# The shared products of a paired down projection stored by ScalarE and summed DRAM to DRAM, the last pair in eight plain products, and an own weight buffer for the first block

## The chip, the cores and the metric

The kernel runs on one core of a Trainium2 chip. The metric is the device time of one execution in microseconds (us), and of several runs the median counts. Besides the timed runs there is one execution that the hardware profiler recorded; every duration of a single instruction below is from it.

## The reference

One layer of a bidirectional encoder, for a prompt of 256 tokens and a sample of 512 with the same weights. Three mixers (a state space model, differential attention, attention into a memory) are gated, projected and added to `x`; then a feed-forward part follows, and only that part is different in its order of work after the change.

```python
D_MODEL = 1024;  D_FF = 2816
def layer(x, mem, ...):
    h = rmsnorm(x, norm_mix_g)
    proj = h @ w_in
    ...                                   # s5_out, diff_out, mem_out
    br = jnp.einsum('blnc,ncd->blnd', branches, w_branch)
    merged = jnp.sum(gates * br, axis=2)
    x = x + merged @ w_out
    h2 = rmsnorm(x, ffn_norm_g)
    g, up = jnp.split(h2 @ w_gate_up, 2, axis=-1)
    return x + (jax.nn.silu(g) * up) @ w_down
```

All data are float32.

## The kernel before

**Precision.** A float32 operand of a matrix product is split into a high and a low part of a format that TensorE takes at a faster rate; ScalarE makes the high part by a copy, VectorE the low one by a subtraction. Each product is then three matmuls, high x high, low x high and high x low (helper `mm3`, lines 798 to 800). So every matmul of the kernel shows one of these three lines, and one tells the stages apart by the tiles' names.

**The feed-forward part.** The 768 tokens are worked as one. The 2816 hidden columns make 11 blocks of 256 (`NFB` = 11). Block 0 is computed plainly, segment by segment, while the normed rows of the last stage are still arriving: `first` (gate and up), then `down_first`, whose PSUM banks are added into the residual tiles `x1` (named `x_0` to `x_5`, one for 128 tokens; line 1486 before). The names there: `fa` is the block's activation, `hidh` its high part, `fs` a staging tile, `flo` the low part of the right factor T2.

Blocks 1 to 10 compute gate and up (`block`) by the Strassen-Winograd scheme: seven products of half-size matrices in place of eight. The sums of weight quarters for it (`ws`, then `wh_S`, `wl_S` after the split) are GpSimd's additions, lines 578 to 585, in `_split_w`. Their raw weights `wr` are loaded by SP into a pool of three tiles; the split halves `wh`, `wl` live in pools of four.

**The down projection in pairs.** The hidden blocks are taken two at a time, (1,2) to (9,10), so that the pair's 512 hidden rows can be cut in two as well and `down_pair` can use seven products (each 3 banks x 2 halves x 3 = 18 matmuls of 512 columns, tile `dn`). With A the activations (token halves by block) and B the weights, the left factors are A11, A12, A22 and the sums S1 to S4 (`ls`, and after the split `lS1h`, `lS1l` and so on, lines 1493 and 1494); the right ones are B11, B21, B22 and T1 to T4, which `_split_d` makes in two tiles `z` and `x` (named `wt...z`, `wt...x`) with ScalarE's negated copies and GpSimd's adding DMAs from `w_down`.

Four of the products go into one quarter of the output each. Three, A11·B11 ("1"), S2·T2 ("6") and S1·T1 ("5"), belong to several quarters. They are the same quarters in every pair, so these products are summed over the pairs in DRAM and added into `x1` once, in `down_sums` ahead of the last pair. On the way there, ScalarE copies a bank to a tile `de` (line 1543), and GpSimd issues the DMA (line 1549) that stores it, or from the second pair on adds it:

```python
gp.dma_start(p_scr[key][t], e[t], **({"accum_op": add} if fb > 1 else {}))
```

The `de` tiles come from a pool of three, which the tile `ft` of the gate's tanh uses too. In the last pair (`last`) there are no later sums: GpSimd issues twelve DMAs that add the `de` tiles straight into the residual tiles (`x<-de`, lines 1559 and 1574), and the output is stored from there by SP (line 1520).

**What sets the order.** A scheduler with a simulated timeline chooses the order of instructions on each engine. An engine then works its queue strictly in that order; a DMA that GpSimd issues stands in GpSimd's queue among its additions. Instructions marked with `keep_in_program_order` stay as written. Weights are fetched by a list (`W.add` fills it, `W.get` takes the next).

Of the kernel before, what the change touches and what calls it, by code (L numbers as in the profile page):

```python
# [487 lines left out]
TOK = 768  # L488
# [16 lines left out]
class WStream:  # L505
# [90 lines left out]
    def _split_d(self, i, h, kind):  # L596
# [16 lines left out]
        elif h == 0:  # L613
            add(self.x, b11)
            self._right(i, "T2", self.x)
            self._right(i, "T1", self.z)
            self._right(i, "B21", r)
        else:
            minus(self.x, self.x)
            add(self.x, b21)  # L620
            self._right(i, "T4", self.x)
            self._right(i, "B22", r)
# [47 lines left out]
def hybrid_block(ctx, tc, A, outs, consts):  # L670
# [48 lines left out]
    cp.tile([128, 32], F32, name="gapc")  # L719
# [41 lines left out]
    for fb in range(NFB):  # L761
        for what in ("gate", "up"):
            W.add(cols("w_gate_up", 256 * fb + (DFF if what == "up" else 0)), 8, 256, "w" if fb else None)
        if fb == 0:
            W.add(wd[:, 0:2, :], 2, 1024)
        elif fb % 2 == 0:
            for b, kind in ((fb - 1, "d"), (fb, "e")):
                W.add([wd[:, 2 * b : 2 * b + 2, 512 * c : 512 * c + 512] for c in range(2)], 4, 512, kind)


    def rsqrt(x, n, tag, bufs=4):
# [3 lines left out]
        y = sm.tile([128, n], F32, name=uid("rqy"), tag=tag, bufs=bufs)  # L775
# [101 lines left out]
    p_scr = {k: [dr.tile([128, 512], F32, name=f"p_scr{k}{t}") for t in range(3)] for k in "165"}  # L877
# [287 lines left out]
    def qk_units(h):  # L1165
        w = W.get()
        r = q2.tile([128, TILES, 256], F32, name=uid("qkraw"), tag="qkraw")
        ss = sm.tile([128, TILES * 4], F32, name=uid("qkss"), tag="qkss")
# [273 lines left out]
    def block(what, fb):  # L1442
# [29 lines left out]
        if what == "up" and fb % 2 == 0:  # L1472
            W.ahead(W.next + 1)
# [16 lines left out]
    def left(key, src):  # L1490
# [4 lines left out]
        L[key] = hi, lo  # L1495

# [6 lines left out]
    def down_begin(fb):  # L1503
# [3 lines left out]
        left("S3", left_sum(None, a[:, :, 0:HT], a[:, :, HT:TOK], sub))  # L1507
# [5 lines left out]
    def into(r, c, y, op=add, done=False, pin=False):  # L1513
        for t in range(3):
            o = out_block(r, c, t)
            i = v.tensor_tensor(out=o, in0=o, in1=y[t], op=op)  # L1516
            if pin:
                tc.keep_in_program_order(i)
# [3 lines left out]
    def down_pair(fb, last):  # L1522
# [8 lines left out]
        def prod(l, r):  # L1531
            (lh, ll), (rh, rl) = L.pop(l), R.pop(r)
            ps = [(psd if t else env.psb)("dn") for t in range(3)]
            for t in range(3):
                sl = slice(128 * t, 128 * t + 128)
                for k in range(2):
                    mm3(ps[t], lh[:, k, sl], ll[:, k, sl], rh[:, k], rl[:, k], k == 0, k == 1)
            return ps

        def copies(ps):  # L1540
            e = [ft_.tile([128, 512], F32, name=uid("de"), tag="ft") for t in range(3)]
            for t in range(3):
                act.activation(e[t], ps[t], AF.Copy)
            return e

        def keep(key, ps):
            e = copies(ps)
            for t in range(3):
                gp.dma_start(p_scr[key][t], e[t], **({"accum_op": add} if fb > 1 else {}))


        p1 = prod("A11", "B11")
# [3 lines left out]
        if last:  # L1556
            e = copies(p1)
            for t in range(3):
                gp.dma_start(out_block(0, 0, t), e[t], accum_op=add)
        else:  # L1560
            keep("1", p1)
        p7 = prod("S3", "T3")
        left("S1", s1)
        into(1, 1, p7, pin=last)
        if last:
            into(1, 0, p7)
        p6 = prod("S2", "T2")
        left("A12", a12)
        if last:
            for t in range(3):  # L1570
                v.tensor_tensor(out=e[t], in0=e[t], in1=p6[t], op=add)
            for r, c in ((1, 1), (1, 0), (0, 1)):
                for t in range(3):
                    gp.dma_start(out_block(r, c, t), e[t], accum_op=add)  # L1574
        else:
            keep("6", p6)
        p5 = prod("S1", "T1")
        left("A22", a22)
        left("S4", left_sum(s2, a12, s2, sub))
        if last:  # L1580
            into(0, 1, p5)
            into(1, 1, p5, done=True)
        else:
# [290 lines left out]
```

## Time and profile before

| what | value |
|---|---|
| runs | 1806.58, 1807.51, 1813.25 us; median 1807.51 |
| profiled execution | 1811.89 us, of which the span of instructions is 1810.1 |
| mean granted TensorE clock | 0.988 |
| block 0 of the feed-forward part | up to about 1347 us |
| the five pairs' `dn` windows begin at | 1391.8, 1480.2, 1572.6, 1665.4, 1755.6 us |
| the last matmul begins at | 1799.0 us |

Rows of the profile are read so. A row of an event has its start, its duration, engine, line, operation, and what it writes and reads (`out<-in`); in square brackets stands how long the engine had been idle and what ended that. A row of waits has the engine, the instruction that waited, after the arrow what it waited for, then the total time, the number of waits and the longest. A row of a window has its bounds, its length, and then for each engine (TensorE, its weight loads, VectorE, ScalarE, GpSimd, SyncE) the busy time and the number of instructions, then the mean granted clock (1.00 is full), the share of time in which the DMA engines moved data, and GB/s. If only one tile is asked for, the engines' columns hold that tile's instructions alone. `x3` behind an event means that three like ones follow one another.

### The profile page before, as it was taken

What the parts mean: (1) busy time and instruction counts of PE and PEld (TensorE: products, weight loads), DVE (VectorE), ACT (ScalarE), POOL (GpSimd) and SP (SyncE); (2) the same over time, 40 slices, a digit from 0 to 9 for tenths busy, and PEclk for the clock granted to TensorE, in tenths of its full rate; (3) what the DMA queues carried; (4) which work ended last, traced back from release to release, by engine and by line L of the source; (5) the groups of instructions that cost most, each with busy time, mean ns of one, the idle gap of its engine ahead of it and who ended that gap; (6) DMA issues with size and microseconds to landing.
All of it is one profiled execution on the core that took longest, in us unless ns stands there. A gap on an engine that the chain in (4) does not pass through costs nothing. (4 is left out here: it accounts for less than half of the span.)

```text
span 1810.1 us, 29578 instructions
## 1 busy us (share of the span) xinstructions
PE 1757.0 (97%) x11196; PEld 1615.4 (89%) x11196; DVE 1315.8 (73%) x2431; ACT 929.1 (51%) x1906; POOL 281.2 (16%) x308
## 2 busy tenths in 40 slices
PE   8999999999999989999999999999989999999986
PEld 8999988999999989999988888888879898989885
DVE  7655658799998678778865444434798787877786
ACT  7454544776666357777664442322435454444432
POOL 0000000000000011101100110000142525243532
PEclk9999999999999999999999999999999999999998
DMA  7232755665565487445932644321314355454656
GB/s 250 71 105 83 136 130 143 152 156 130 148 157 131 124 191 188 90 97 116 226 108 82 223 146 140 114 76 54 87 58 119 120 122 117 113 123 105 137 135 150
DMA packets 210430, 233.31 MB, mean 129 GB/s; under 512 B 59056, under 2 KB 168880, under 8 KB 210288
## 3 DMA queue, kind: packets, MB, share of 16 engines
q1 hardware_dynamic: 178512, 149.63, 27.9%
q0 software_dynamic: 30624, 78.66, 21.2%
q10 hardware_dynamic: 1152, 3.15, 0.5%
q8 instruction: 88, 1.44, 0.3%
q14 instruction: 54, 0.44, 0.1%
HBM read 158.96 MB, written 42.01 MB: 111 GB/s over the span
## 5 line engine op out<-in xcount | busy, mean ns | idle before, releaser
L638 ACT ACTIVATE wh<-wr 128x1024 fp32r<-128x1024 f32 x126 | 142.9, 1134 | 72.8 <-PE br L799 27.9
L644 DVE TENSOR_TENSOR wl<-wr,wh 128x1024 fp32r<-128x1024 f32 x80 | 106.5, 1332 | 74.3 <-ACT wh L638 73.2
L798 PE MATMUL gl<-Hhi,wh 128*128 128x256 f32 (+1 forms) x384 | 132.2, 344 | 1.3 <-ACT glt L1108 1.3
L800 PE MATMUL gl<-Hhi,wl 128*128 128x256 f32 (+1 forms) x384 | 128.9, 336 | 0.0
L799 PE MATMUL gl<-Hlo,wh 128*128 128x256 f32 (+1 forms) x384 | 128.8, 336 | 0.0
L642 POOL DMA_DIRECT2D wl<-wr x46 | 40.1, 871 | 519.2 <-ACT wl L641 484.0
L798 PE MATMUL qk<-wh,Hhi 128*128 128x256 f32 x384 | 108.7, 283 | 4.1 <-ACT qksq L1174 4.1
L799 PE MATMUL qk<-wl,Hhi 128*128 128x256 f32 x384 | 108.8, 283 | 0.0
L800 PE MATMUL qk<-wh,Hlo 128*128 128x256 f32 x384 | 108.8, 283 | 0.0
L798 PEld LDWEIGHTS gl<-Hhi,wh 128*128 128x128 f32 x384 | 72.2, 188 | 8.6 <-ACT glt L1108 1.5
L800 PEld LDWEIGHTS gl<-Hhi,wl 128*128 128x128 f32 x384 | 72.0, 188 | 8.1
L799 PEld LDWEIGHTS gl<-Hlo,wh 128*128 128x128 f32 x384 | 72.3, 188 | 7.2
L798 PEld LDWEIGHTS qk<-wh,Hhi 128*128 128x128 f32 x384 | 73.4, 191 | 5.2 <-ACT qksq L1174 4.5
L1274 DVE TENSOR_REDUCE nm<-sc 128x1 f32<-128x512 f32 (+1 forms) x96 | 57.2, 599 | 24.2 <-PE sc L1269 22.9
L800 PEld LDWEIGHTS qk<-wh,Hlo 128*128 128x128 f32 x384 | 73.5, 191 | 0.7
L799 PEld LDWEIGHTS qk<-wl,Hhi 128*128 128x128 f32 x384 | 73.4, 191 | 0.5
L563 ACT ACTIVATE wh_S<-ws 128x512 fp32r<-128x512 f32 x70 | 41.6, 626 | 53.0 <-PE up L799 20.3
L1276 ACT ACTIVATE p<-sc,nm 128x512 f32<-128x512 f32 (+1 forms) x96 | 59.0, 616 | 12.0 <-DVE nm L1274 11.6
L564 DVE TENSOR_TENSOR wl_S<-ws,wh_S 128x512 fp32r<-128x512 f32 x70 | 55.1, 812 | 9.8 <-ACT wh_S L563 9.6
L1627 ACT ACTIVATE glr<-glr 128x768 f32<-128x768 f32 x24 | 20.3, 846 | 65.6 <-DMA glr<-gl_scr 64.1
L798 PE MATMUL v<-wh,Hhi 128*128 128x256 f32 x192 | 53.9, 281 | 0.0
L799 PE MATMUL v<-wl,Hhi 128*128 128x256 f32 x192 | 53.8, 280 | 0.0
(572 smaller groups left out, 6272.1 us busy)
## 6 DMA issues: line engine op xcount, KB each, us to landing
wr<-in_w_in_dram SPq DMA_DIRECT2D x48, 512.0 KB, 5.3
wl<-wr POOLq DMA_DIRECT2D x46, 512.0 KB, 5.2
wr<-in_w_gate_up_dram SPq DMA_DIRECT2D x44, 512.0 KB, 3.5
wr<-in_w_branch_dram SPq DMA_DIRECT2D x24, 512.0 KB, 4.3
wr<-in_w_down_dram SPq DMA_DIRECT2D x22, 512.0 KB, 4.8
glr<-gl_scr POOLq DMA_DIRECT2D x24, 384.0 KB, 3.8
p_scr<-de POOLq DMA_DIRECT2D x36, 256.0 KB, 6.0
wr<-in_w_mem_kv_dram SPq DMA_DIRECT2D x16, 512.0 KB, 3.8
```

Source lines behind the costliest of these rows:

```text
L563: self.nc.scalar.activation(f(hi), src, AF.Copy)
L564: self.nc.vector.tensor_tensor(out=f(lo), in0=src, in1=f(hi).bitcast(F32), op=ALU.subtract)
L638: self.nc.scalar.activation(hi, r, AF.Copy)
L642: self.nc.gpsimd.dma_start(lo, r.bitcast(F32R), accum_op=ALU.add)
L644: self.sub.tensor_tensor(out=lo, in0=r, in1=hi.bitcast(F32), op=ALU.subtract)
L798: pe.matmul(ps, wh, xh, start=start, stop=False)
L799: pe.matmul(ps, wh, xl, start=False, stop=False)
L800: pe.matmul(ps, wl, xh, start=False, stop=stop)
L1274: v.tensor_reduce(out=nm[:, m : m + 1], in_=ps, axis=AX.X, op=ALU.max, negate=True)
L1276: act.activation(pm[:, 0:n], ps, AF.Exp, bias=nm[:, m : m + 1], accum_out=s1s[:, tt : tt + 1] if m == 0 else s2)
L1627: act.activation(g, g, AF.Tanh, scale=0.5)
```

## The change

1. **Shared products** (`keep`). ScalarE copies a bank to one `de` tile at a time and issues its store itself, for the first pair into the sums `p_sum`, later into a fresh DRAM tile; GpSimd then issues a DMA that adds that DRAM tile to the sum, DRAM to DRAM. The order of the seven products is new: 1, 7 (S3·T3), 6, A12·B21, 5, A22·T4, S4·B22.
2. **Last pair** (`down_last`). Eight plain products in place of seven, both blocks accumulated in the same bank, so each quarter has one bank for each 128 tokens, which VectorE adds to `x1` and SP stores. Its weights are only split, without sums.
3. **Block 0's down weights** are split into a buffer of their own (`W.extra`) for the first half, in place of the pool of four; T1's scratch comes from another pool.
4. Small: `gapc` is gone, `qkss` and the `rsqrt` results have fewer buffers, B21 is made ahead of T1, and the subtraction for the pairs (`x(1,0) -= x(1,1)`, at block 2) keeps its written place.

```diff
@@ in _split_d: the weights of a pair, first half of its second block
             self._right(i, "T2", self.x)
+            self._right(i, "B21", r)
             self._right(i, "T1", self.z)
-            self._right(i, "B21", r)
...
         if fb == 0:
-            W.add(wd[:, 0:2, :], 2, 1024)
+            W.add(wd[:, 0:2, :], 2, 1024, "x")
         elif fb % 2 == 0:
             for b, kind in ((fb - 1, "d"), (fb, "e")):
-                W.add([wd[:, 2 * b : 2 * b + 2, 512 * c : 512 * c + 512] for c in range(2)], 4, 512, kind)
+                if fb == NFB - 1:
+                    W.add(wd[:, 2 * b : 2 * b + 2, :], 2, 1024)
+                else:
+                    W.add([wd[:, 2 * b : 2 * b + 2, 512 * c : 512 * c + 512] for c in range(2)], 4, 512, kind)
...
-    p_scr = {k: [dr.tile([128, 512], F32, name=f"p_scr{k}{t}") for t in range(3)] for k in "165"}
+    p_sum = {k: dr.tile([128, 3, 512], F32, name=f"p_sum{k}") for k in "165"}
...
-        def keep(key, ps):
-            e = copies(ps)
-            for t in range(3):
-                gp.dma_start(p_scr[key][t], e[t], **({"accum_op": add} if fb > 1 else {}))
+        def keep(key, ps):
+            d = p_sum[key] if fb == 1 else dr.tile([128, 3, 512], F32, name=uid("p_scr"))
             for t in range(3):
+                e = ft_.tile([128, 512], F32, name=uid("de"), tag="ft")
+                act.activation(e, ps[t], AF.Copy)
+                act.dma_start(d[:, t], e)
+                if fb > 1:
+                    gp.dma_start(p_sum[key][:, t], d[:, t], accum_op=add)
+        keep("1", prod("A11", "B11"))
         s1 = left_sum(None, a21, a22, add)
         s2 = left_sum(None, s1, a11, sub)
         left("S2", s2)
...
+        into(1, 1, prod("S3", "T3"))
+        left("A12", a12)
+        keep("6", prod("S2", "T2"))
         left("S1", s1)
...
+        into(0, 0, prod("A12", "B21"))
         left("A22", a22)
+        keep("5", prod("S1", "T1"))
         left("S4", left_sum(s2, a12, s2, sub))
...
+        into(1, 0, prod("A22", "T4"))
+        into(0, 1, prod("S4", "B22"))
+
+    def down_last(fb):
+        a, b = act_in.pop(fb), act_in.pop(fb + 1)
+        w = [W.get(), W.get()]
+        for r in range(2):
+            h = slice(HT * r, HT * r + HT)
+            x = [L.pop("A11") if r == 0 else left("A21", a[:, :, h]), left("A2", b[:, :, h])]
+            ps = [banks(), banks()]
+            for i in range(2):
+                for c in range(2):
+                    y = [(lambda k, j=j: w[i](k, 512 * c, 512)[j]) for j in range(2)]
+                    rows_times(ps[c], x[i], y, i == 0, i == 1)
+            for c in range(2):
+                into(r, c, ps[c], done=True)
...
         if fb == 2:
-            into(1, 0, [out_block(1, 1, t) for t in range(3)], sub)
+            for t in range(3):
+                o = out_block(1, 0, t)
+                tc.keep_in_program_order(v.tensor_tensor(out=o, in0=o, in1=out_block(1, 1, t), op=sub))
```

The order of the instructions is the same on every engine up to the feed-forward part. Three places show how it moves.

ScalarE in the second pair, before: the copies of a product are followed by other work, and GpSimd issues the stores.

```order
L1493 ACTIVATE lA12h_16564<-fa_16137 128x768
L592 ACTIVATE wh_T_16418<-wt73x 128x1024
L1543 ACTIVATE de_16568<-dn_16543 128x512
L1543 ACTIVATE de_16569<-dn_16544 128x512
L1493 ACTIVATE lA22h_16598<-fa_16137 128x768
L592 ACTIVATE wh_B_16422<-wr_1_16300 128x1024
L1543 ACTIVATE de_16570<-dn_16545 128x512
L1543 ACTIVATE de_16607<-dn_16577 128x512
L1493 ACTIVATE lS4h_16603<-ls_16500 128x768
```

And in the changed kernel:

```order
L1496 ACTIVATE lS1h_16582<-ls_16512 128x768
L592 ACTIVATE wh_T_16419<-wt73x 128x1024
L1555 ACTIVATE de_16570<-dn_16548 128x512
L1556 DMA p_scr_16569<-de_16570 128x512
L1555 ACTIVATE de_16574<-dn_16549 128x512
L1496 ACTIVATE lA22h_16610<-fa_16138 128x768
L592 ACTIVATE wh_B_16423<-wr_1_16301 128x1024
L1555 ACTIVATE de_16578<-dn_16550 128x512
L1556 DMA p_scr_16569<-de_16574 128x512
L1556 DMA p_scr_16569<-de_16578 128x512
L1496 ACTIVATE lS4h_16649<-ls_16514 128x768
```

The stores (DMA) now stand in ScalarE's queue, one or two instructions behind their copies, and `lS4h` stands behind the last store of the second shared product.

GpSimd in the same place, before: the stores alternate with the sums `ws` of the next gate block's weights.

```order
L1549 DMA p_scr_175<-de_16508 128x512
L578 TENSOR_TENSOR ws_16449<-wr_0_16309,wr_1_16414 128x512
L579 TENSOR_TENSOR ws_16450<-ws_16449,wr_0_16309 128x512
L583 TENSOR_TENSOR ws_16451<-wr_0_16309 128x512
L1549 DMA p_scr_176<-de_16568 128x512
L1549 DMA p_scr_177<-de_16569 128x512
```

And in the changed kernel:

```order
L1558 DMA p_sum_172<-p_scr_16499 128x512
L578 TENSOR_TENSOR ws_16450<-wr_0_16310,wr_1_16415 128x512
L1558 DMA p_sum_172<-p_scr_16499 128x512
L579 TENSOR_TENSOR ws_16451<-ws_16450,wr_0_16310 128x512
L583 TENSOR_TENSOR ws_16452<-wr_0_16310 128x512
L1558 DMA p_sum_172<-p_scr_16499 128x512
L1558 DMA p_sum_173<-p_scr_16569 128x512 x3
L1558 DMA p_sum_174<-p_scr_16635 128x512 x2
L585 TENSOR_TENSOR ws_16453<-wr_1_16415,ws_16451 128x512
```

In place of the stores stand the additions from DRAM to DRAM; `ws` line 585 stands behind eight of the nine.

VectorE in the first block, before: between the splits stand the subtractions of line 1516, the third of them directly ahead of `flo`.

```order
L1516 TENSOR_TENSOR x_4_12317<-x_4_12317 128x512
L564 TENSOR_TENSOR wl_A_14900<-wr_0_14671,wh_A_14899 128x512
L1456 TENSOR_TENSOR fs_15046<-fs_15046,gate_15062 128x384
L564 TENSOR_TENSOR wl_A_15025<-wr_1_14871,wh_A_15024 128x512
L1516 TENSOR_TENSOR x_5_12318<-x_5_12318 128x512
L792 TENSOR_TENSOR flo_14039<-fB_14792,fhi_14038 128x4x384
```

And in the changed kernel:

```order
L1489 TENSOR_TENSOR x_5_12311<-x_5_12311,dn_14984 128x512
L564 TENSOR_TENSOR wl_A_15026<-wr_1_14870,wh_A_15025 128x512
L564 TENSOR_TENSOR wl_A_15026<-ws_15020,wh_A_15025 128x512
L1458 TENSOR_TENSOR fs_15047<-fs_15047,gate_15080 128x384
L794 TENSOR_TENSOR flo_14032<-fB_14791,fhi_14031 128x4x384
```

The subtractions are gone from there (they stand some 50 instructions later, ahead of the first pair); the split of block 0's down weights, which stood among the `fB` sums, now stands ahead of them, right behind the output projection's additions to `x`.

77 lines of the change are left out of this document (24 added, 53 removed).

## The prediction

> **What bounds the kernel now.** I read the page first. TensorE is busy almost all the span, so the time can fall only where TensorE idles, runs at a lower clock, or has finished.
>
> ```profile
> span 1810.1 us, 29578 instructions
> PE 1757.0 (97%) x11196; PEld 1615.4 (89%) x11196; DVE 1315.8 (73%) x2431; ACT 929.1 (51%) x1906; POOL 281.2 (16%) x308
> ```
>
> The code differs only from the feed-forward part on, so the second view is TensorE's waits from 1230 us to the end (total, times, longest):
>
> ```profile
> PE dn L798 <- ACT lS4h L1493: 10.4, 4, 3.5
> PE up L798 <- ACT fs L1461: 3.9, 1, 3.9
> PE dn L798 <- ACT lS2h L1493: 3.3, 1, 3.3
> PE dn L798 <- DVE x L1486: 2.5, 1, 2.5
> PE gate L799 <- DVE flo L792: 2.3, 1, 2.3
> PE up L798 <- DVE fs L1456: 1.2, 3, 0.6
> ...
> PE dn L798 <- ACT hidh L1419: 0.6, 1, 0.6
> ```
>
> They fall into three places: `lS4` in the four early pairs, `hidh`, `x`, `flo` and `fs` L1456 in the first block, `fs` L1461 and `lS2h` in the last pair. Idling also costs clock. Third view: stretches behind three of these waits (length, busy time by engine, granted clock, DMA share, GB/s), each at half clock:
>
> ```profile
> 1344.50:1347.90 3.40, 2.98 (x10) 2.48 (x10) 3.40 (x4) 0.63 (x1) 2.69 (x3) 0.50 0.00 0
> 1508.30:1511.70 3.40, 3.40 (x10) 2.63 (x10) 3.40 (x7) 2.27 (x4) 2.09 (x3) 0.51 0.83 160
> 1778.00:1781.40 3.40, 3.40 (x10) 2.62 (x9) 3.40 (x6) 0.49 (x1) 0.00 (x0) 0.50 0.00 0
> ```
>
> Each costs up to 1.7 us (half of 3.40). The first follows an idle of 2.3 us, the second one of `lS4h` (3.5 at most), the third 3.3. The Trainium skill ("TensorE: Matmul & The Clock Gate", HAM oscillation) asks for no idle gaps above about 3.4 us. By it only the longest waits, 3.5 and 3.9, would cost clock, and my forecast would be about 5 us higher (in the two early places three slow stretches fewer to win); the trace shows the slow stretch behind a gap of 2.3 too, and I go by the trace.
>
> **Early pairs.** The same view for the tile `dn` alone, over the four pairs, and TensorE alone for one `up` block (the columns are then its busy time, clock, DMA share and GB/s):
>
> ```profile
> 1391.80:1422.20 30.40, 29.43 (x126) 23.32 (x126) 6.06 (x10) 5.11 (x9) 1.00 0.49 146
> 1480.20:1514.60 34.40, 31.01 (x126) 24.42 (x126) 6.56 (x10) 5.23 (x9) 0.95 0.67 128
> 1572.60:1607.40 34.80, 30.94 (x126) 24.59 (x126) 6.56 (x10) 5.23 (x9) 0.95 0.66 126
> 1665.40:1699.80 34.40, 30.78 (x126) 24.47 (x126) 6.57 (x10) 5.22 (x9) 0.95 0.67 127
> ```
>
> ```profile
> 1621.80:1636.60 14.80, 14.72 (x84) 1.00 0.22 71
> ```
>
> 126 matmuls take 29.43 us at full clock, 0.2336 each, a product of 18 takes 4.2; a gate or up product of 12 takes 14.72/7 = 2.1. The four pairs lose 0.9, 4.9, 5.3 and 4.9 us to it, 16.0 together. Why `lS4h` is late, in pair three, first ScalarE, then GpSimd:
>
> ```profile
> 1598.11 0.60 ACT L1543 ACTIVATE de<-dn 128x512 f32<-128x512 f32 x1 [8.78 <-DMA p_scr<-de]
> 1598.60 0.83 ACT L1493 ACTIVATE lS4h<-ls 128x768 fp32r<-128x768 f32 x1
> ```
>
> ```profile
> 1577.56 3.21 POOL L1549 DMA_DIRECT2D p_scr<-de  x3
> 1589.38 1.87 POOL L578 TENSOR_TENSOR ws<-wr,wr 128x512 f32<-128x512 f32 x1 [8.62 <-DMA wr<-in_w_gate_up_dram]
> 1593.81 2.63 POOL L1549 DMA_DIRECT2D p_scr<-de  x3
> ```
>
> There are three `de` buffers. ScalarE needs one back, GpSimd's queue holds the store behind `ws`, and `ws` waits for a weight load. `lS4h` stands behind that copy on ScalarE. In the changed kernel ScalarE issues the store itself, so no buffer waits for GpSimd. Its nearest price is the other store that ScalarE issues (issue time min/median/max in ns, then landing); beside it SP's stores of the output:
>
> ```profile
> L1329 ACTq DMA_DIRECT2D br_scr<-do x8: 326/326/401, 755.2 to 999.0; - x8
> DMA to landing us min/median/max: 2.3/3.2/4.9
> ```
>
> ```profile
> L1520 SPq DMA_DIRECT2D out_dram<-x x12: 332/462/1325, 1789.9 to 1806.1; - x12
> ```
>
> Landing in 2.3 to 4.9 us, a buffer is free well before the next group of copies, a product of 4.2 us or more later. The issues cost 9 x 0.33 = 3 us of ScalarE per pair, beside 8.8 us of idle that go away; `S4` is now the last product, 4.2 us later than it could start. What is late next is `lS2h`: two issues and their waits for the copies, about 1 us, now stand ahead of it.
>
> ```profile
> 1579.40 0.85 ACT L1493 ACTIVATE lS2h<-ls 128x768 fp32r<-128x768 f32 x1 [0.46 <-DVE ls L1500]
> ```
>
> It ended at 1580.25; its product begins two products after 1572.7, at about 1581.1. It had 0.8 us of slack and another 0.5 us in its own wait for `ls`, so I expect 0 to 0.5 us of wait per pair and take 0.3, 1.2 in all; if the issues took 1.3 us each, as the longest on SP did, it would be near 2 us per pair. GpSimd's sums for the next gate block now stand behind waits for ScalarE's stores, the last for the first two tiles of S1·T1, whose product ends 21 us into the pair, so near 24; the S4 weights that they give are used only after 29.4 us and the next gate's first five products of 2.1. That cover is 16 us. Gain: 16.0 - 1.2 = 14.8 us; bounds 6 and 16.
>
> **First block.** ScalarE's rows there show one wait feeding the next:
>
> ```profile
> 1300.04 1.06 ACT L638 ACTIVATE wh<-wr 128x1024 fp32r<-128x1024 f32 x1 [0.73 <-PE gate L799]
> 1308.76 0.63 ACT L563 ACTIVATE wh_A<-wr 128x512 fp32r<-128x512 f32 x1 [2.92 <-DMA wr<-in_w_gate_up_dram]
> 1312.18 0.63 ACT L563 ACTIVATE wh_S<-ws 128x512 fp32r<-128x512 f32 x1 [1.41 <-POOL ws L578]
> 1316.21 0.61 ACT L1419 ACTIVATE hidh<-fa 128x512 fp32r<-128x512 f32 x1
> ```
>
> The down weights' split waits for a buffer that the gate product holds; their raw buffer is free only then, so the next weights load late, GpSimd sums late, and `hidh` is queued behind it. With an own buffer the split stands, in the order, ahead of the gate product, and loads and sums move ahead with it. VectorE is the other limit:
>
> ```profile
> 1299.30:1343.30 44.00, 38.71 (x184) 32.99 (x183) 43.96 (x47) 17.64 (x25) 17.39 (x7) 1.00 0.18 55
> 1341.54 1.75 DVE L792 TENSOR_TENSOR flo<-fB,fhi 128x1536 fp32r<-128x1536 f32 x1
> ```
>
> ```profile
> L1516 DVE TENSOR_TENSOR x<-x x3: 679/682/1766, 1335.1 to 1339.8; 128x512 f32<-128x512 f32 x3
> ```
>
> It works 43.96 of 44 us up to the `flo` for which TensorE waits. The change takes from it three subtractions (two of 0.7, one of 1.77) and a split (`wl` beside the 1.06 of its `wh`, so about as long again): 4 us, more than the 2.3 of that wait, and `flo` gets one `up` product of 2.1 us as cover in the order. The subtractions return ahead of the first pair, where TensorE waits for no VectorE instruction. At stake are 0.6 + 2.5 + 2.3 + 1.0 of waits and 1.7 of clock, 8.1 us. I take 6: of the 2.5 us for a bank about 1 to 2 stay, because VectorE still clears the banks between the splits. Bounds 0 (GpSimd's earlier sums slow VectorE while `rows` feeds the gate, as may be what made one subtraction take 1.77) and 8.
>
> **Last pair.** Eight products instead of seven: 18 more matmuls, 18 x 0.2336 = +4.2 us. Gone are GpSimd's four additions of weights (one `wt91z`, three `wt91x`) and its twelve `x<-de`. The end now, TensorE's last row and VectorE's:
>
> ```profile
> 1799.00 0.39 PE L800 MATMUL dn<-wh_B,lS4l 128*128 128x512 f32 x1
> 1804.23 1.88 DVE L1516 TENSOR_TENSOR x<-x,dn 128x512 f32<-128x512 f32 x3 [1.42 <-DMA x<-de]
> ```
>
> TensorE ends at 1799.4, VectorE waits for the accumulations till 1806.1, and 4.0 us later the span ends. After: the last bank is added at once (0.7) and the same 4.0 follow, 4.8 with the gap between. Ahead of that, gate and up of the last block:
>
> ```profile
> 1728.70:1744.40 15.70, 15.27 (x84) 1.00 0.36 116
> 1752.86 0.52 ACT L1411 ACTIVATE ft<-fs 128x384 f32<-128x384 f32 x1 [4.27 <-DVE de L1597]
> 1755.89 1.06 ACT L592 ACTIVATE wh_T<-wt91x 128x1024 fp32r<-128x1024 f32 x1 [2.51 <-PE up L800]
> ```
>
> From 1728.7 the span needs 81.4 us more. After: a gate and an up block of 14.7 each, 144 x 0.2336 = 33.6, so 63.0, a remaining wait of 2.0 and the end of 4.8: 69.8. Gain 11.6. The 2.0 is my choice between 0 and the 3.9 + 1.7 that stand there now: `ft` still waits for `down_sums` to give its buffer back, but the last loads of those sums no longer share the queues with the accumulations, and the new weights need only a copy and a subtraction. Bounds 8 and 14.
>
> **Sum.** 14.8 + 6 + 11.6 = 32.4 us, 1.8%. The profiled execution took 1811.89 us, 4.4 above the median of 1807.51 and inside the spread of the three; from the median, 1775; from its own time, 1779.5. The smaller attention buffers (`qkss`, `qkrs`) I cost at nothing: no instruction ahead of the feed-forward part changes place, and a buffer comes round two heads later.
>
> **Rivals.**
> - The last pair keeps its wait of 5.6 us in place of 2.0, with the sums' loads late again: 1779; with the end unhurried too, 1783. For it: `ft` stands on the same buffers.
> - The first block gives nothing: 1781.
> - ScalarE becomes late: 2 us of `lS2h` wait and a slow stretch of 1.7 in four pairs, 4 x 3.4 = 13.6 less: 1789. For it, a slack below 1 us; against it, issues of 0.33 us.
> - The DMA engines fill. With nine accumulating stores they were busy 0.67 x 34.4 = 23.0 us in pair two, with nine plain ones 0.49 x 30.4 = 14.9 in pair one, 0.9 more for each; nine plain stores more, at that much again, come to 31.1 of 29.4 us. If a weight of the pair is then 3 us late, with a slow stretch behind it, each of three pairs loses 4.7: 1789. The Trainium skill ("DMA: Bandwidth & Descriptors", Issuing engines are not separate DMA queues) speaks for this one: a second issuing engine saves only issue time. Against it, the overflow has four gate and up blocks, 59 us, at shares like the 0.22 and 0.36 shown.
> - On the other side: the DRAM-to-DRAM accumulation, which no row shows, is so slow that GpSimd's queue never drains and the weights' additions stand behind it. From the list of issues (number, size, median to landing):
>
> ```profile
> p_scr<-de POOLq DMA_DIRECT2D x36, 256.0 KB, 6.0
> wt79x<-in_w_down_dram POOLq DMA_DIRECT2D x3, 512.0 KB, 6.4
> ```
>
> Two blocks and a pair take 88 us; four weight additions at 6.4 leave 62.4 for nine transfers, so it binds if each holds the queue for more than 6.9 us, and costs 9 us per pair for every further microsecond. Beyond 8.1 us three pairs lose the 32 us, and the kernel is slower: 1832 at 9. Against it, the stores land 6.0 after the issue with three in flight, about 2 each.
>
> **How the numbers follow.** The forecast as worked out, 0.52; last pair 0.13; first block 0.12; ScalarE 0.10; DMA engines 0.08; queue 0.03; hardly any change 0.02. The range 1765 to 1794 runs from all bounds good (16 + 8 + 14 gives 1769.5, less 4.5, the spread of the profiled run) to the two 1789 cases joined by the last pair's 4. What this measurement can tell from no change is 0.5%, 9 us: only the queue case and part of the last are not faster.
>
> **What would show it.** Right: no 8 us wait of a `de` copy for a store; `dn` windows of pairs two to four near 29.8 us at clock 1.00; no `flo` or `hidh` wait, the first block's `ws` ahead of its gate product's end; `out_dram` ending within 5 us of TensorE's last matmul. Wrong: a wait for `lS2h` over 1 us in every pair, ScalarE's store landing beyond 6 us, `ws` waiting for p_scr stores long enough that a gate product waits for `wl_S`, or a half-clock stretch in the last pair.

## The result, and the profile after

The changed kernel took 1783.3 us (median of four runs, 1780.15 to 1785.17) against 1808.72 of the kernel before on the same chip: ratio 0.9854, 95% interval 0.983 to 0.9879. It is faster by 25 us; the forecast was 32 (1775, range 1765 to 1794). The time lies in the range, but one of the three terms of the forecast failed.

The profiled execution took 1780.15 us. First its span and TensorE's row, then TensorE's waits from 1230 us to the end (total, times, longest):

```profile
span 1778.4 us, 29549 instructions
PE 1748.8 (98%) x11214; PEld 1611.2 (91%) x11214; DVE 1307.2 (74%) x2409; ACT 917.3 (52%) x1894; POOL 252.0 (14%) x283
```

```profile
PE dn L800 <- ACT lS2h L1496: 7.3, 3, 3.2
PE gate L800 <- DVE fs L1458: 2.0, 2, 1.6
PE dn L800 <- DVE x L1489: 1.0, 1, 1.0
PE up L800 <- DVE fs L1458: 0.8, 1, 0.8
PE nT L829 <- DVE flo L794: 0.5, 1, 0.5
PE gate L800 <- DVE x L1489: 0.2, 1, 0.2
```

`lS4h`, `hidh`, `fs` L1461 and the 2.3 us for `flo` are gone. What stands at the top is new: `lS2h`, the instruction that the prediction named as late next, but with 7.3 us instead of 1.2. The four pairs' windows, for the tile `dn` alone (columns as before):

```profile
1379.50:1410.70 31.20, 29.08 (x126) 23.40 (x126) 7.33 (x12) 5.17 (x9) 1.00 0.54 154
1468.70:1497.70 29.00, 28.94 (x126) 23.44 (x126) 6.53 (x10) 5.17 (x9) 1.00 0.75 175
1555.80:1586.90 31.10, 29.07 (x126) 23.38 (x126) 6.53 (x10) 5.17 (x9) 1.00 0.75 175
1645.00:1678.90 33.90, 30.66 (x126) 24.49 (x125) 6.63 (x10) 5.28 (x9) 0.95 0.76 173
```

Only pair two runs through. Pairs one and three wait 2.0 us each, pair four 3.2 and then runs at a lower clock. ScalarE at the start of pair four shows what `lS2h` stands behind:

```profile
1648.88 1.06 ACT L592 ACTIVATE wh_T<-wt85x 128x1024 fp32r<-128x1024 f32 x1 [9.85 <-DMA wt85x<-in_w_down_dram]
1652.20 0.58 ACT L1555 ACTIVATE de<-dn 128x512 f32<-128x512 f32 x1
1655.68 0.83 ACT L1496 ACTIVATE lS2h<-ls 128x768 fp32r<-128x768 f32 x1
```

ScalarE idles 9.85 us for the T2 weights, which land 3.8 us into the pair, and its whole queue waits with it, `lS2h` too. In the kernel before, and in pair two here, they land 0.4 to 0.5 us into the pair. The stores that ScalarE issues are the small part: from the start of T2's split to the end of `lS2h` it is 7.6 us here, in pair two as in pair four, and 7.1 us in the kernel before and in the run with GpSimd's stores below. With T2 punctual that is still in time.

For a sum by place, TensorE's timeline is cut at three points: the last matmul of the output projection (`wo`), the first of pair one, the last of pair four.

| profiled execution | `wo` to pair one | pairs one to four with the blocks between | from there to the end |
|---|---|---|---|
| before | 121.5 | 307.9 | 110.4 |
| changed | 114.2 | 299.4 | 99.5 |
| gain | 7.3 | 8.5 | 10.9 |
| forecast | 6 | 14.8 | 11.6 |

Together 26.7 us. The two profiled executions differ by 31.7; the other 5.0 lie ahead of the feed-forward part, where the order is the same, and where the end of `wo` lay anywhere from 1265.3 to 1270.9 us in the executions of this study, with and without the change.

### The profile page after: what moved, and what is told of

Read it like the earlier page. It is cut to its first block, busy times and chain, and to the rows that moved or that the text cites. A ratio compares the mean times of both kernels' runs of the same rounds, so it can differ in the third digit from the quotient of the medians.

```text
span 1778.4 us, 29549 instructions
## 1 busy us (share of the span) xinstructions
PE 1748.8 (98%) x11214; PEld 1611.2 (91%) x11214; DVE 1307.2 (74%) x2409; ACT 917.3 (52%) x1894; POOL 252.0 (14%) x283
## 5 line engine op out<-in xcount | busy, mean ns | idle before, releaser
L638 ACT ACTIVATE wh<-wr 128x1024 fp32r<-128x1024 f32 x130 | 146.8, 1130 | 74.4 <-PE br L801 27.5
L644 DVE TENSOR_TENSOR wl<-wr,wh 128x1024 fp32r<-128x1024 f32 x84 | 111.0, 1322 | 75.4 <-ACT wh L638 74.8
L564 DVE TENSOR_TENSOR wl_S<-ws,wh_S 128x512 fp32r<-128x512 f32 x70 | 56.2, 823 | 15.6 <-ACT wh_S L563 15.4
L1278 ACT ACTIVATE p<-sc,nm 128x512 f32<-128x512 f32 (+1 forms) x96 | 59.1, 617 | 13.3 <-DVE nm L1276 12.8
```

Of the source, the lines that this page charges most:

```text
L564: self.nc.vector.tensor_tensor(out=f(lo), in0=src, in1=f(hi).bitcast(F32), op=ALU.subtract)
L638: self.nc.scalar.activation(hi, r, AF.Copy)
L644: self.sub.tensor_tensor(out=lo, in0=r, in1=hi.bitcast(F32), op=ALU.subtract)
L1278: act.activation(pm[:, 0:n], ps, AF.Exp, bias=nm[:, m : m + 1], accum_out=s1s[:, tt : tt + 1] if m == 0 else s2)
```

## The experiments

The theory drawn from this profile (A): the additions from DRAM to DRAM slow the weight loads behind a pair; the stream of weights is then late for the next one. The rival (B): ScalarE's own store issues make `lS2h` late. A second question was whether ScalarE's stores or the new order of the products had removed the `lS4h` waits (C: the order).

**No additions.** In `keep` (the sums of all pairs but the first are left out of the output):

```diff
                 act.dma_start(d[:, t], e)
-                if fb > 1:
-                    gp.dma_start(p_sum[key][:, t], d[:, t], accum_op=add)
```

> The changed kernel without the 27 additions from DRAM to DRAM, with every other instruction in the same order; the sums then hold the first pair's products only, so the output lacks the others. Theory A (carried lateness): the burst of these additions after a pair delays the gate's weight loads (11 to 13 us instead of 4 to 6) and with them the weights' stream; at the next pair the T2 weights land 2 to 3 us later, and ScalarE's whole queue, lS2h in it, stands behind their split. Then the lS2h waits of pairs three and four (2.0 and 3.2 us, and a half-clock stretch worth 1.7) go, pair one keeps its 2.0, and the time falls by 5 to 8 us. Theory B (the stores that ScalarE issues make lS2h late by themselves): the stores stay, so all three waits stay and the time is within 1 us.

1777.54 us, ratio 0.9809 (0.9787 to 0.9831). Its wait for `lS2h`:

```profile
PE dn L800 <- ACT lS2h L1496: 2.1, 1, 2.1
```

Only pair one still waits; pairs two to four take 29.1, 28.9 and 28.9 us. So B is out for pairs three and four, since the stores are all there; for pair one, which has no additions ahead of it, the run with GpSimd's stores below decides.

**Small additions.** The same instruction with `p_sum[key][0:8, t], d[0:8, t]`, so that only 8 of 128 rows are summed.

> As the changed kernel, but each of the 27 additions from DRAM to DRAM moves 8 of 128 rows (the rest of the sums is left out). They stand in GpSimd's queue as before and wait for ScalarE's stores as before, but carry a sixteenth of the bytes. If theory A's delay is traffic on the DMA engines, the weight loads after a pair take 4 to 6 us again and pairs three and four lose their waits as without any addition (5 to 8 us less). If it is the place in GpSimd's queue (the ws of line 585 behind eight of nine additions), loads are fast but ws comes as late as before, and the waits stay within 0.5 us.

1777.55 us, ratio 0.981 (0.9789 to 0.9831), as without any; both ratios are clear of the changed kernel's repeat below (0.9841 to 0.9868). Pairs two to four take 29.1, 29.5 and 28.9 us; pair one waits 3.1 us and takes 33.8. The DMA issues in a stretch of 16 or 17 us from 15 us into pair two on (number, KB each, median us to landing), of the changed kernel and then of this one:

```profile
p_sum<-p_scr POOLq DMA_DIRECT2D x7, 256.0 KB, 9.2
p_scr<-de ACTq DMA_DIRECT2D x5, 256.0 KB, 4.5
wr<-in_w_gate_up_dram SPq DMA_DIRECT2D x2, 512.0 KB, 12.3
```

```profile
wr<-in_w_gate_up_dram SPq DMA_DIRECT2D x3, 512.0 KB, 3.9
p_scr<-de ACTq DMA_DIRECT2D x5, 256.0 KB, 3.7
p_sum<-p_scr POOLq DMA_DIRECT2D x8, 16.0 KB, 4.5
```

With a sixteenth of the bytes the first two weight loads take 3.9 and 6.6 us (the third 3.5), with the full additions 11.8 and 12.7. In GpSimd's queue the additions stand in the same places, but for one per pair that stands one place earlier. On VectorE one weight split and one addition per pair change places, in this run and in the one before it. It is the traffic, not the queue. The Trainium skill ("DMA: Bandwidth & Descriptors", Issuing engines are not separate DMA queues) says that transfers of all issuing engines share the same DMA engines; these rows agree: SP's loads pay for GpSimd's additions.

**S2 early.** S1, S2 and the split of S2 are written ahead of the up block's last product, and the T2 weights' splits are queued behind them:

```diff
         if what == "up" and fb % 2 == 0:
+            if fb < NFB - 1:
+                a, b = act_in[fb - 1], act_in[fb]
+                s1 = left_sum(None, a[:, :, h2], b[:, :, h2], add)
+                s2 = left_sum(None, s1, a[:, :, h1], sub)
+                left("S2", s2)
...
+                with tc.issue_after(last_split[0]), tc.issue_after(last_split[1]):
+                    W.ahead(W.next + 1)
             W.ahead(W.next + 1)
...
```

> The changed kernel with S1, S2 and the split of lS2 computed in the up block and queued ahead of the split of the T2 weights on ScalarE and VectorE (all else kept, the output complete). Theory A says that lS2h is late only because it stands behind the T2 split on ScalarE, while the T2 split itself, 5 to 6 us into the pair at the latest, is in time for the third product at 8.4: all three waits (7.3 us) and the half-clock stretch (1.7) go, 1774 to 1776 from 1783. Rival: the third product then waits for the T2 weights, or a later piece of ScalarE's queue is late in place of it (lS1h, lA22h or a copy), and the sum of TensorE's waits in the pairs stays above 4 us.

1780.86 us, ratio 0.9826 (0.9801 to 0.9851). `lS2h` is out of the list, but the waits did not go away:

```profile
PE dn L800 <- ACT wh_T L592: 3.6, 3, 1.5
PE dn L801 <- DVE wl_T L593: 1.6, 3, 0.5
```

The rival of that expectation came true: 5.2 us in the pairs, above its 4. Pair one is mended (28.8 us), the other three now wait for the split of T4's weights, ahead of A22·T4. T2's weights are punctual there (0.3 to 0.8 us), but their split stands behind S2 and starts 3.3 us into the pair. The copy and GpSimd's DMA that make T4 follow it; in pairs two to four T4 lands 20.5 to 20.9 us into the pair, in pair one, which has no additions, 16.6. Moving S2 alone is no cure where the additions still run.

**GpSimd's stores.** The changed kernel with the shared products stored as before the change:

```diff
-            d = p_sum[key] if fb == 1 else dr.tile([128, 3, 512], F32, name=uid("p_scr"))
...
                 act.activation(e, ps[t], AF.Copy)
-                act.dma_start(d[:, t], e)
-                if fb > 1:
-                    gp.dma_start(p_sum[key][:, t], d[:, t], accum_op=add)
+                gp.dma_start(p_scr[key][t], e, **({"accum_op": add} if fb > 1 else {}))
```

> The changed kernel with the shared products stored as before the change: GpSimd issues the stores, accumulating from the second pair, no DRAM to DRAM additions; new order of products, last pair and own buffer kept. The prediction's step says that the copies of de then wait again some 8 us for GpSimd's queue and S4, S1 or A22 come late: 3 to 5 us more in each of pairs two to four, 1790 to 1798. Rival: the new order of the products (S4 last) already hides that wait, and the ScalarE stores were worth nothing: within 2 us of the changed kernel, or faster, as less traffic delays the weights.

1780.88 us (1774.16 to 1783.71), ratio 0.9822 (0.9792 to 0.9852): not slower than the changed kernel, where that expectation's first reading asked for 1790 to 1798. Here are the rows on the `de` copies' idle time, of the changed kernel and of this one (total, times), then this one's waits of TensorE in the pairs:

```profile
ACT de L1555: 2.2, 5
```

```profile
ACT de L1554: 31.4, 15
```

```profile
PE dn L800 <- ACT lS2h L1496: 2.1, 1, 2.1
PE dn L800 <- DVE x L1489: 1.0, 1, 1.0
PE dn L800 <- ACT de L1554: 1.0, 1, 1.0
```

The copies wait 31.4 us for stores, as they did before the change (38.8), and it costs TensorE 1.0 us, because S4 is now the last product and nothing due stands behind them. Pair one waits 2.1 us for `lS2h` without a store in ScalarE's queue, as long as the changed kernel with them, so B is out for pair one too. The pairs with the blocks between take 293.6 us (changed 299.4), the end 97.5 (99.5). The run's times spread too far to rank the two; below, a run on one chip with the changed kernel ranks them with one more edit in pair one.

**The parts alone.** The changed kernel was run again with three others on one chip, the first two of them made from the kernel before.

> The changed kernel, not edited, beside the three that follow on one chip, as their measure: 1780 to 1786, ratio to the kernel before 0.983 to 0.988, with lS2h waits in pairs one, three and four.

1785.31 us, ratio 0.9854 (0.9841 to 0.9868). Again 8.2 us for `lS2h`, in pairs one, three and four.

Order only, in the kernel before: the new sequence of products for pairs one to four (the last pair keeps the old one), with `keep` as it was. Lines that only make the left factors are left out here.

```diff
+            if i < len(self.src) - 1:
+                self._right(i, "B21", r)
+                self._right(i, "T1", self.z)
...
+        if not last:
+            keep("1", prod("A11", "B11"))
...
+            into(1, 1, prod("S3", "T3"))
...
+            keep("6", prod("S2", "T2"))
...
+            into(0, 0, prod("A12", "B21"))
...
+            keep("5", prod("S1", "T1"))
...
+            into(1, 0, prod("A22", "T4"))
+            into(0, 1, prod("S4", "B22"))
+            return
```

> The kernel before with one part of the change: the new order of the products in the first four pairs (S4 last, B21 ahead of T1); GpSimd stores as before, no ScalarE stores, no DRAM to DRAM additions, last pair and first block as before. Theory C (the order is what mended the pairs): the de copies still wait some 30 us for GpSimd's stores, but nothing that TensorE needs stands behind them in time; the lS4h waits (10.4 us) and the slow stretches go, 11 to 16 us less than before, ratio 0.991 to 0.994. The prediction's reading (the wait of the de copies makes S4 late, ScalarE's stores cure it): other left factors behind the same copies are late in place of S4, and no more than 5 us are won.

1796.05 us, ratio 0.9912 (0.9899 to 0.9926): 16 us less. No wait of `lS4h` or `lS2h` in the first four pairs; 28.8, 28.8, 28.8 and 30.2 us. Their stretch takes 290.8 us, 17.1 less than before. Theory C holds, and the reading that only the stores mend the pairs (no more than 5 us here) does not.

Stores only, in the kernel before, with the old order of the products:

```diff
-            e = copies(ps)
+            d = p_sum[key] if fb == 1 else dr.tile([128, 3, 512], F32, name=uid("p_scr"))
             for t in range(3):
-                gp.dma_start(p_scr[key][t], e[t], **({"accum_op": add} if fb > 1 else {}))
+                e = ft_.tile([128, 512], F32, name=uid("de"), tag="ft")
+                act.activation(e, ps[t], AF.Copy)
+                act.dma_start(d[:, t], e)
+                if fb > 1:
+                    gp.dma_start(p_sum[key][:, t], d[:, t], accum_op=add)
```

> The kernel before with the other half: ScalarE copies one bank at a time and stores it itself, and GpSimd adds DRAM to DRAM; old order of the products, last pair and first block as before. The prediction's reading: no de copy waits for a store, and lS4h comes in time, 10 to 16 us less than before. Theory C with carried lateness: the lS4h waits go as well since ScalarE no longer waits, but the traffic makes the weights of pairs three and four late and lS2h waits of 2 to 3 us stand there instead, 6 to 12 us less than before.

1800.14 us, ratio 0.9931 (0.9917 to 0.9945): 12.5 us less. The stretch of the pairs takes 292.2 us, 15.7 less than before: ScalarE's stores alone also cure the `lS4h` waits, as forecast. The `lS2h` waits of 2 to 3 us that the second reading put in pairs three and four are there, but small: 0.4 and 0.8 us. The end, though, takes 114.3 us, 3.9 more, of which 2.4 lie in waits of a gate block for VectorE:

```profile
PE gate L798 <- DVE fs L1456: 2.4, 3, 1.6
```

So each half alone removes nearly all that there was to win in the pairs, and they don't add up: the changed kernel, with both and with the new first block, wins 8.5 us there.

GpSimd's stores, and S2 early in the first pair only: the edit of the GpSimd stores, and that of S2 with

```diff
-            if fb < NFB - 1:
+            if fb == 2:
```

> The changed kernel with GpSimd's accumulating stores in place of ScalarE's and of the DRAM to DRAM additions, and with S1, S2 and the split of lS2 ahead of the T2 split in the first pair alone. With theory C and carried lateness: the waits of the four pairs fall from 7.3 to about 1 us, 5 to 9 us less than the changed kernel on the same chip, 1774 to 1779 and the fastest of these. Rival: the weights of T2 are the next to be late in pair one, or the time is the same within 2 us as that of the changed kernel since TensorE waits elsewhere instead.

1775.58 us, ratio 0.9801 (0.9788 to 0.9814), 10 us less than the changed kernel on the same chip and the fastest of the study. The pairs take 28.8, 29.2, 28.8 and 28.8 us. From the end of `wo` on, the profiles take 516.1 us (changed kernel again), 505.3 (GpSimd's stores alone, on another chip) and 501.8 here, so by them the stores are the larger part of the gain. All that is left of TensorE's waits from 1230 us to the end:

```profile
PE dn L800 <- DVE x L1496: 1.0, 1, 1.0
PE up L800 <- DVE fs L1458: 0.8, 1, 0.8
PE nT L829 <- DVE flo L794: 0.5, 1, 0.5
PE gate L800 <- DVE fs L1458: 0.5, 1, 0.5
PE gate L800 <- DVE x L1496: 0.2, 1, 0.2
```

The next three share another chip. Own buffer only, in the kernel before (with the smaller attention buffers):

```diff
-            W.add(wd[:, 0:2, :], 2, 1024)
+            W.add(wd[:, 0:2, :], 2, 1024, "x")
...
+    W.extra = tuple(fhctx.enter_context(tc.tile_pool(name="wx" + w, bufs=1)) for w in "hl")
...
-            t1 = whole(new("fB11"), "B11")
+            t1 = whole(fa.tile([128, 4, HT], F32, name="fB11", tag="fa"), "B11")
```

> The kernel before with one part of the change: the first half of block 0's down weights in a buffer of its own (with the smaller attention buffers that make room for it and T1's scratch from the other pool); stores, order of products, last pair and the place of the three subtractions as before. The prediction's step: the hidh, x and part of the flo waits go, block 0 ends 4 to 7 us earlier against the gate of the first segment. If the weights' stream is the next limit (as the lS2h wait of pair one in the changed kernel suggests), pair one starts ahead of its T2 weights and gives 2 to 4 us back. Together 2 to 6 us less than before, ratio 0.9965 to 0.999.

1809.59 us, ratio 0.9987 (0.9978 to 0.9997), 2 us. `wo` to pair one takes 120.0 us, 1.6 less than before. The waits moved (TensorE, the first block up to 1362 us):

```profile
PE up L797 <- DVE fs L1455: 3.6, 3, 2.7
PE dn L797 <- DVE x L1485: 1.0, 1, 1.0
PE gate L797 <- DVE x L1485: 0.2, 1, 0.2
```

Last pair only, in the kernel before: `down_last` of the change and the plain loads of the last two blocks' weights.

```diff
-            down_pair(fb - 1, fb == NFB - 1)
+            if fb == NFB - 1:
+                down_last(fb - 1)
+            else:
+                down_pair(fb - 1, False)
```

> The kernel before with one part of the change: the last pair in eight plain products with outputs stored straight from VectorE's additions; all else as before. The prediction's term for it alone: 11.6 us less (8 to 14), 1799 to 1804 with before at 1812, ratio 0.992 to 0.9955. Rival: the wait of the last up block for ft and the down sums stays, since the sums come as late as before, and only 6 to 8 us are won.

1797.86 us, ratio 0.9917 (0.9903 to 0.993): 15 us less, the end 97.1 us instead of 110.4. More than the forecast's 11.6; the rival with the wait for `ft` is out, no such wait is left.

The changed kernel with the old order of the products:

```diff
+            self._right(i, "T1", self.z)
             self._right(i, "B21", r)
-            self._right(i, "T1", self.z)
...
+        p6 = prod("S2", "T2")
         left("A12", a12)
-        keep("6", prod("S2", "T2"))
...
+        keep("6", p6)
+        p5 = prod("S1", "T1")
...
+        keep("5", p5)
         into(0, 0, prod("A12", "B21"))
...
-        keep("5", prod("S1", "T1"))
...
         into(1, 0, prod("A22", "T4"))
```

> The changed kernel with the old order of the products in the first four pairs (S1T1 fourth, A12B21 fifth, T1 ahead of B21), ScalarE's stores and the DRAM to DRAM additions kept. ScalarE's stores alone, in the old order, left lS2h waits below 0.8 us per pair. If it is the new order together with the additions that makes the weight loads slow and T2 late, the waits of pairs three and four fall below 1 us each and the time is 3 to 7 us below the changed kernel's 1785. If it is the earlier start of pair one (own buffer), carried from pair to pair by a stream that has no reserve, the waits stay: 6 to 9 us in all, within 2 us of the changed kernel.

1785.88 us, ratio 0.985 (0.9834 to 0.9866): no gain in the time. The waits for `lS2h` in pairs three and four fall to 0.4 and 1.1 us as the first reading said, and pair one waits 2.6. The four pairs together take 120.2 us (changed 125.1), but the gate and up blocks between them 2.1 us more, of which 1.8 stand in one wait of a gate block. The 2.8 us that the profile still shows for that stretch do not appear in the time.

```profile
PE dn L800 <- ACT lS2h L1496: 4.1, 3, 2.6
PE gate L800 <- DVE fs L1458: 2.1, 2, 1.6
PE gate L800 <- DVE x L1521: 1.8, 1, 1.8
```

In the new order two loads behind a pair are slow (11.3 to 12.7 us behind pairs two and three; 8.9 to 12.9 in the repeat), in the old one a single one (10.2 to 11.4 us behind pairs two to four). The order sets where the additions' traffic hurts, not whether.

Own buffer and the late subtractions, in the kernel before. Edit: that of the own buffer, and

```diff
-            into(1, 0, [out_block(1, 1, t) for t in range(3)], sub)
+            for t in range(3):
+                o = out_block(1, 0, t)
+                tc.keep_in_program_order(v.tensor_tensor(out=o, in0=o, in1=out_block(1, 1, t), op=sub))
```

> The kernel before with the own buffer as in the run before it, and with the three subtractions of line 1516 kept behind what is written ahead of them, as the change has it; stores, order of products and last pair as before. The first block's instructions then stand as in the changed kernel. If the subtractions are the larger part of the first block's gain, the wait of up for fs (2.7 us at the longest with the buffer alone) and the slow stretch behind it go, and the gate of block 1 begins about 85 us after the output projection's last matmul, as in the changed kernel (92.4 before, 90.8 with the buffer alone). Pair one then starts ahead of its T2 weights and gives about 2 us back: 4 to 7 us less than before in all, ratio 0.996 to 0.998. Rival: the subtractions were no more than filling, and it stays at 0.9987.

1805.46 us, ratio 0.996 (0.9946 to 0.9973), 7 us less than before. The wait for `fs` of the run with the own buffer alone is gone, `wo` to pair one takes 114.2 us as in the changed kernel. So of the 7.3 us there, the buffer alone brings 1.6 and the place of three subtractions, with the buffer there, 5.7. In that 5.7 is a choice of the scheduler: with the subtractions gone it also puts some `fs` and `fa` ahead of weight splits on VectorE, and no run takes the two apart. And pair one now waits 2.0 us for `lS2h` and takes 33.9 us (30.5 with the buffer alone).

## Why the prediction was right and where it was wrong

The direction and the place of each gain were right, and two of three terms came out near their size, one of them by luck. The forecast from profile to profile was 1779.5 us and the profiled execution took 1780.15; that this nearly meets is luck, since 5.0 of its 31.7 us lie where nothing was changed. Of the prediction's own signs, the waits of `de` copies are gone (2.2 us in all), `hidh` is gone, and the last store of the output lands 2.7 us behind TensorE's last matmul. The windows of pairs two to four were to be near 29.8 us at full clock; only pair two was.

**First block: 6 forecast, 7.3 measured.** The size is right. Its split among causes was not: the own buffer came first in the text and brings least. VectorE's full queue was the limit, as the 43.96 of 44 us said; three subtractions less on it, and the order that this allowed, were worth more than the buffer. What the forecast did not count is what pair one gives back. T2's weights land 0.4 to 0.9 us into pair one with the old first block (before, order only, stores only), and 2.6 to 3.7 us into it in all runs with the new one. Counted from the end of `wo`, the pair begins 7.3 us sooner (114.2 instead of 121.5), the weights land only 4 to 5 us sooner (116.9 to 118.0 instead of 121.9). With the order or the stores alone `lS2h` is waited for 0 and 0.3 us there, with the new block 2.0 to 3.1 us wherever S2 stands in its old place.

**Early pairs: 14.8 forecast, 8.5 measured.** This term failed, at two steps. The first is "I expect 0 to 0.5 us of wait per pair" for `lS2h`. The slack of 0.8 us was read rightly (it ends 8.2 us into pair two, just in time), and the issue time of 0.33 us too. But what comes ahead of `lS2h` on ScalarE is first of all the split of T2, and it was taken as punctual. The second is "That cover is 16 us" for GpSimd's sums behind the additions: the delay was not taken up by the next gate block. Counted from the first slow load in pair two, the fourth load was issued 9 us later than in the run without additions, the fifth and sixth still 4.4 us later, and T2 landed 89.6 us after the start of pair two instead of 87.6. Each raw tile has to be summed and split before its buffer takes the next load, so the delay came down to the next pair as 2 to 3 us. The runs without additions and with small ones showed that it is the additions' traffic: in the new order of the products pairs three and four took 65.0 us together with it and 57.8 without (59.6 with it in the old order), the slow stretch included, which is more than the whole miss of 6.3. The rival "The DMA engines fill" named the resource and the kind of harm, a weight some 3 us late, and had 0.08; it said pairs two to four, and it was three and four. Its sum was too high: the engines were busy for 0.75 of pair two, not for more than all of it; they filled behind it (0.93 of the 16 us shown above, 0.47 without additions).

The mechanism of the term, that ScalarE's own store frees the buffer, was right in itself (15.7 us alone). That the order of the products does the same alone (17.1) the prediction missed. It mentioned that S4 comes last now and took no consequence from it: with the order changed, the buffer wait was harmless and the stores bought nothing but traffic.

**Last pair: 11.6 forecast, 10.9 measured,** from three errors that nearly cancel, which is luck. The remaining wait of 2.0 did not come: the part alone wins 13.3 us in its profile. The end took 4.1 us from TensorE's last matmul, not 4.8. But the last gate block, taken at 14.7, became slower, 18.0 us instead of the 15.6 before:

```profile
1707.80:1726.00 18.20, 15.90 (x86) 14.36 (x84) 18.05 (x28) 5.74 (x10) 7.72 (x4) 1.00 0.31 102
```

VectorE works 18.05 of 18.2 us there. It splits the block's weights and adds the shared sums at once. With no additions, small additions or GpSimd's stores the end takes 97.5 to 97.8 us, with the full additions 99.5 to 100.0 (and 3.9 us more in the kernel before with the stores alone). The run with S2 early, with all additions, had 97.6, so it is not the additions as such. That late weights push their splits among the sums fits all of these, but no run took it apart, so the cause stays open. At the very end the last bank's addition begins 0.4 us behind the start of the last matmul, and the span ends 4.1 us behind that.

```profile
1773.89 0.39 PE L802 MATMUL dn<-wh,lA2l 128*128 128x512 f32 x1
1774.32 0.69 DVE L1521 TENSOR_TENSOR x<-x,dn 128x512 f32<-128x512 f32 x1 [0.67 <-PE dn L802]
```

**The slow side** did not come: seven additions issued within one stretch land 9.2 us after their issue while overlapping, nowhere near 6.9 us each. With small additions, which leave that queue nearly as it is, the time is that without any, so GpSimd's queue was not the limit.

## What to carry to other kernels

A wait that a trace shows on the path can be hidden by order as well as removed, as here; before paying for its removal (here 27 more transfers), ask whether the consumer can simply come later. Bytes that are added off the path are paid by whatever shares the DMA engines and has no reserve, here weight loads that go from 4 to 7 us up to 12, and the bill may arrive a whole period later, in another queue. When a change removes slack from one stage, look at which stream was sized to the old length: its next deadline gives part of the gain back.

## What the runs showed of the hardware that was not expected

The length of a single idle does not decide whether TensorE's clock falls. Behind a wait of 2.09 us in pair one (the run without additions) there is a slow stretch, and the pair takes 32.8 us; behind waits of 2.08 (GpSimd's stores) and 2.05 (changed kernel) there is none, and it takes 31.1. A wait of 1.92 in pair one brought one (last pair only), and waits of 2.48 in pair three (changed kernel again) and 3.34 in the last pair (own buffer and late subtractions) did not. The Trainium skill ("TensorE: Matmul & The Clock Gate", HAM oscillation) asks for no gap above about 3.4 us; here shorter ones cost clock, some of them and not others.

The traces show what decides between them. Within each profile, the slow stretches start whole multiples of 3.413 us apart (in the kernel before at 1344.49, 1508.33 and 1600.49 us, which are 48 and 27 such steps), as if time were cut into cells of that length. What counts is how much of one cell TensorE idles. TensorE alone (busy time, clock, DMA share, GB/s), for the cells around three of these waits: no additions, GpSimd's stores, and the last pair with own buffer and late subtractions.

```profile
1390.62:1394.03 3.41, 1.51 (x7) 1.00 0.97 182
1394.03:1397.45 3.42, 3.42 (x10) 0.50 0.94 279
```

```profile
1390.10:1393.51 3.41, 1.80 (x8) 1.00 0.98 153
1393.51:1396.92 3.41, 3.41 (x17) 1.00 1.04 363
```

```profile
1765.46:1768.87 3.41, 1.84 (x9) 1.00 1.06 185
1768.87:1772.28 3.41, 1.65 (x7) 1.00 0.55 99
1772.28:1775.70 3.42, 3.42 (x17) 1.00 0.00 0
```

In the first, 1.90 us of one cell are idle, and the next cell runs at half clock; in the second 1.61, and nothing follows. In the third, the long wait falls on two cells with about 1.6 and 1.8 us each. Over the 14 profiles of this study, from 1262 us to the last matmul, each of the 34 cells with 1.90 us of idle or more was followed by a slow one. Of some 2100 with 1.82 us or less none was, but for one that was slow itself. So what a wait costs there hangs on where it falls on the cells, and that changes from execution to execution. The border is no sharp rule for the whole kernel: earlier than that, four cells of 1.4 to 1.85 us were followed by a slow one too, and one of 1.90 was not.
